# Encoder layer on one core: loads of the first three blocks in one order, and the first turning of results later

## The chip, the cores and the metric

One core of a Trainium2 chip runs the whole program. The metric is the device time of one execution in microseconds (us), the median over runs: 1160.44 us before the change (three runs, 1158.86 to 1162.03).

## What is computed

One layer of an encoder on 256 positions with 2048 features, all in float32:

```python
n = rmsnorm(h, norm_mix_w[layer])
proj = n @ w_in[layer]                       # 2048 x 7168: q_a k_a v_a q_r k_r v_r g_r
attn = dilated_mixture_attention(heads(q_a), heads(k_a), heads(v_a), slopes)
ret = bidirectional_retention(heads(q_r), heads(k_r), heads(v_r), ...)
...
h = h + mixed @ w_out[layer]
n2 = rmsnorm(h, norm_ffn_w[layer])
h = h + (jax.nn.silu(n2 @ w_gate[layer]) * (n2 @ w_up[layer])) @ w_down[layer]
return rmsnorm(h, norm_final_w)
```

## The kernel before

The products make up nearly all of the time. Each float32 factor is split into a high and a low part, and a product is three matmuls (high by high, low by high, high by low). The input projection is cut into seven blocks, `in0` to `in6`, each with 1024 output columns (for `in0` 512 of q_a and 512 of k_a). A block is a string of steps, written out in `ORDERS`. "C" is one K tile taken the plain way: one weight tile of 128 x 1024 (512 KB), 12 matmuls of 512 columns. Numbers 1 to 7 are the products of a Strassen-like scheme for four K tiles (Winograd's), 6 matmuls each. "1a" loads three weight tiles (named rawc, raw12, raw22) and forms sums of them: `rawt` = r11 + r12 on VectorE (DVE), and raw12 += raw22 by an accumulating DMA of GpSimd (POOL). "2a" loads another into raw22, which then takes += rawt in the same way. `in0` has 16 C steps, 192 matmuls. `in1` has seven numbered steps and 12 C, 186 matmuls.

Weights come in the order of the steps over SP's DMA queue, into three buffers rawc, two raw12, three raw22 and one rawt. Each tile is copied by ScalarE (ACT) into its high part, and DVE subtracts to get the low part (`halved`, L154 and L157); the results are `ws` tiles, of which there are five. Preparing runs three steps ahead of the matmuls in program order. x comes transposed in eight pairs of K tiles (`need`), is multiplied by the norm's gain and halved; for the first two pairs, sums of the pair's quarters (`pair_sums`, tiles s and sa) feed the numbered steps. The factor of the norm itself is applied to results afterwards: `measure_x` loads x once more in eight pieces (xs, on POOL's queue), ACT squares and sums each, and `factor` turns the sums into r1 (DVE, DVE, POOL).

The letters M, H, T and N in an order are places for other work. M combines the numbered products. In `in1`, H calls `factor` and scales the four parts of `in0` by r1, and each T turns one part (q, then k) with eight transposes on TensorE (PE) into a bank, from where ACT and DVE halve it. N in `in0` starts `measure_x`. `later` is a list of small pieces of work, one taken after each step.

`ch(ins)` ties an instruction to the one before it on the same engine, so that the scheduler keeps that order. Matmuls, ACT's copies, DVE's steps and POOL's DMAs go through it; SP's loads (L250, L267, L411, L418) do not, and the scheduler places them by its own estimate.

Of the kernel before, what the change touches and what calls it, by code (L numbers as in the profile page):

```python
# [9 lines left out]
F32 = mybir.dt.float32  # L10
F32R = mybir.dt.float32r
AF = mybir.ActivationFunctionType
ALU = mybir.AluOpType
# [75 lines left out]
def encoder_layer(ctx: ExitStack, tc: tile.TileContext, xT, x, gains, gain_f, decay, tab, bias, w_st, y):  # L89
# [49 lines left out]


# [63 lines left out]
    class Block:  # L204


        def __init__(self, name, kind, a, sa, end, hooks=(), parts=None, need=None):
            self.name, self.a, self.sa, self.end, self.hooks = name, a, sa, end, {k: list(v) for k, v in dict(hooks).items()}
            self.parts, self.need, self.fine = parts, need, need is not None
            self.banks, self.raws, self.begun, self.left, self.kept, self.share = {}, {}, set(), {}, [], {}  # L210
            self.steps = steps_of(kind)
            for what, n in self.steps:
                for r in {"C": (2, 3, 4, 8), "K": (2, 3), "Z": ()}.get(what, (what,) if isinstance(what, int) else ()):
                    self.left[r] = self.left.get(r, 0) + (3 if what in ("C", "K") else 6)
                if what == "K":
                    for r in (4, 8):
                        self.left[r] += 3
            stream.extend((self, what, n) for what, n in self.steps)
# [29 lines left out]
        def load(self, home):  # L248
            raw = self.raw(home)
            nc.sync.dma_start(raw, next(tiles).rearrange("p (n c) -> p n c", c=NB))  # L250
            return raw
# [6 lines left out]
        def prepare(self, what, m):  # L258
            if self.need:
                for p in ([m // 2] if what == "C" else [2 * m, 2 * m + 1]):  # L260
                    self.need(p)
            if what == "C" and self.fine:
                self.fine = False
                raw, src = self.raw("c"), next(tiles)
                ws = wsp.tile([P, 2, 2, NB], F32R, tag="ws", name=f"ws_{self.name}")
                for n in range(2):
                    nc.sync.dma_start(raw[:, n], src[:, n * NB:(n + 1) * NB])  # L267
                    copy(ws[:, n, 0], raw[:, n])
                    tt(ws[:, n, 1], raw[:, n], ws[:, n, 0].bitcast(F32), ALU.subtract)
                return ws  # L270
            if what == "C":
                return self.halve(self.load("c"))
# [109 lines left out]
    def end_take(block, i, n, bank):  # L382
        block.share[i, n] = ttile(f"part{i}{n}_{block.name}").rearrange(flat)
# [18 lines left out]
    n1, n1_sums = [None] * (KT // 2), [None] * 2  # L402

    def need(p):
        if n1[p] is not None:
            return
        t = ttile(f"x_{p}")
        w = nw[:, 2 * p:2 * p + 2]
        n1[p] = atile(f"n1_{p}")
        if p < 2:  # L410
            nc.sync.dma_start(t, xT[p])  # L411
            for f in range(2):
                copy(t[:, f], t[:, f], scale=w[:, f:f + 1])
            halved(n1[p], t)
            n1_sums[p] = pair_sums(t, f"n1_{p}")
        else:
            for f in range(2):
                nc.sync.dma_start(t[:, f], xT[p][:, f])  # L418
            weighed(n1[p], t, w)

    def measure_x():
# [11 lines left out]
        for n in range(10):  # L433
            later.append(lambda n=n: (n < 8 and fetch(*divmod(n, 2)), n > 1 and take()))
            later.append(lambda: None)
# [202 lines left out]
    for b, sections in enumerate(INPUT + ((None, None),)):  # L638
        hooks = {}
        if b == 0:  # L640
            hooks = {"N": [measure_x]}
# [17 lines left out]
        if sections[0] is not None:  # L659
            prev = Block(f"in{b}", KIND_IN[b], n1, n1_sums, end_take if b == 0 else end_share if b < 3 else end_scaled, hooks,  # L660
                         need=None if b else need)
# [197 lines left out]
```

## Time and profile before

| | |
|---|---|
| median of 3 runs | 1160.44 us |
| profiled execution | 1162.72 us |
| its span | 1160.9 us |
| PE busy | 1133.2 us (98%), 5166 matmuls |
| DVE, ACT, POOL busy | 923.3, 683.3, 106.5 us |
| HBM read | 223.90 MB, 195 GB/s over the span |

Busy time of PE is modelled and includes matmuls that wait for their input, so the pace of matmuls (starts per microsecond) tells more than the share. "Granted clock" is the share of full speed that the throttle allowed PE.

### The profile page before, as it was taken

The page shows a single profiled execution, that of the slowest core. Times are in us where ns is not written, and L with a number is a line of the kernel's source. Part 1 is how long each engine was busy: PE and PEld are TensorE (multiplying, and loading weights), DVE is VectorE, ACT ScalarE, POOL GpSimd, SP SyncE. Part 2 cuts the span into 40 slices and gives each one's busy share as a digit, 9 for nine tenths or more (in the row PEclk, how much of TensorE's full clock was granted, in tenths as well). Part 3 has the DMA queues.
Part 4 walks back from the last instruction along what each step waited for, and adds up shares of the span by engine and source line. Part 5 has one row for each costly group of instructions (what it writes and reads, how often), then busy time and mean ns, then how long its engine had stood idle before and what let it go on. Part 6 is the DMA issues. An engine that isn't in the chain of part 4 may idle for free.

```text
span 1160.9 us, 14434 instructions
## 1 busy us (share of the span) xinstructions
PE 1133.2 (98%) x5166; PEld 937.8 (81%) x5166; DVE 923.3 (80%) x1052; ACT 683.3 (59%) x842; POOL 106.5 (9%) x135
## 2 busy tenths in 40 slices
PE   8989999999999999999999999999999999999996
PEld 6768888888888887778888888788888888888785
DVE  4658786754577686789998888899989888999895
ACT  4665564745466465656656555576666555666553
POOL 1010100000001110010000021000100202000011
PEclk9899999999999999999999999999999999999999
DMA  8875755455577877669988899988898899889785
GB/s 289 264 209 166 252 181 182 145 171 192 170 250 228 248 201 197 221 191 263 266 248 243 275 261 258 306 240 249 256 274 236 235 323 262 273 260 278 230 233 148
DMA packets 79400, 272.04 MB, mean 234 GB/s; under 512 B 9184, under 2 KB 10720, under 8 KB 79328
## 3 DMA queue, kind: packets, MB, share of 16 engines
q1 hardware_dynamic: 62640, 220.76, 54.7%
q0 software_dynamic: 15968, 49.29, 22.9%
q10 hardware_dynamic: 720, 1.07, 0.3%
q8 instruction: 40, 0.66, 0.2%
q14 instruction: 32, 0.26, 0.1%
HBM read 223.90 MB, written 2.10 MB: 195 GB/s over the span
## 4 chain that ended last, share of the span: by engine, by line
PE 79%; DVE 7%; DMA 6%; ACT 3%; issue 2%; POOL 0%; SPq 0%; DVEq 0%; POOLq 0%; ACTq 0%
PE p_gu L231 32%; PE p_in L231 21%; PE p_d L231 17%; PE p_o L231 5%; DMA rawc_in<-in_w_st 3%; DMA rawc_gu<-in_w_st 2%; DVE ws_gu L157 2%; ACT ws_in L154 1%; DVE ws_in L157 1%; PE pt_h L356 1%; DVE ws_d L157 1%; DMA rawc_o<-in_w_st 1%; ACT ws_gu L154 1%; DMA x<-in_xT 1%; DVE ws_o L157 1%
## 5 line engine op out<-in xcount | busy, mean ns | idle before, releaser
L231 PE MATMUL p_gu<-ws_gu,n 128*128 128x512 f32 x1482 | 351.5, 390 | 3.3 <-ACT ws_gu L154 2.6
L231 PEld LDWEIGHTS p_gu<-ws_gu,n 128*128 128x128 f32 x1482 | 277.7, 188 | 62.3 <-ACT ws_gu L154 3.7
L231 PE MATMUL p_in<-ws_in,n 128*128 128x512 f32 x1284 | 307.9, 397 | 6.2 <-ACT ws_in L154 6.2
L231 PEld LDWEIGHTS p_in<-ws_in,n 128*128 128x128 f32 x1284 | 242.6, 191 | 57.3 <-ACT ws_in L154 7.7
L157 DVE TENSOR_TENSOR ws_in<-rawc_in,ws_in 128x1024 fp32r<-128x1024 f32 (+1 forms) x107 | 129.0, 1212 | 68.2 <-ACT ws_in L154 67.0
L231 PE MATMUL p_d<-ws_d,h 128*128 128x512 f32 x708 | 168.0, 390 | 0.9 <-DVE ws_d L157 0.9
L157 DVE TENSOR_TENSOR ws_gu<-rawc_gu,ws_gu 128x1024 fp32r<-128x1024 f32 x113 | 137.6, 1221 | 28.0 <-ACT ws_gu L154 26.5
L231 PEld LDWEIGHTS p_d<-ws_d,h 128*128 128x128 f32 x708 | 132.7, 188 | 29.3 <-DVE ws_d L157 1.3
L154 ACT ACTIVATE ws_gu<-rawc_gu 128x1024 fp32r<-128x1024 f32 x113 | 118.7, 1055 | 54.9 <-PE p_gu L231 28.4
L154 ACT ACTIVATE ws_in<-rawc_in 128x1024 fp32r<-128x1024 f32 (+1 forms) x107 | 111.6, 1047 | 66.1 <-PE p_in L231 44.2
L231 PE MATMUL p_gu<-ws_gu,sa_n 128*128 128x512 f32 x504 | 128.7, 391 | 0.0
L231 PEld LDWEIGHTS p_gu<-ws_gu,sa_n 128*128 128x128 f32 x504 | 93.9, 188 | 19.4 <-DVE ws_gu L157 0.4
L157 DVE TENSOR_TENSOR ws_gu<-raw_gu,ws_gu 128x1024 fp32r<-128x1024 f32 x84 | 102.4, 1220 | 2.4 <-ACT ws_gu L154 1.1
L154 ACT ACTIVATE ws_gu<-raw_gu 128x1024 fp32r<-128x1024 f32 x84 | 88.5, 1053 | 23.1 <-PE p_gu L231 18.5
L157 DVE TENSOR_TENSOR ws_d<-rawc_d,ws_d 128x1024 fp32r<-128x1024 f32 x54 | 65.7, 1220 | 17.6 <-ACT ws_d L154 17.0
L154 ACT ACTIVATE ws_d<-rawc_d 128x1024 fp32r<-128x1024 f32 x54 | 57.1, 1057 | 37.2 <-PE p_d L231 20.1
L154 ACT ACTIVATE ws_gu<-rawt_gu 128x1024 fp32r<-128x1024 f32 x42 | 44.3, 1055 | 56.4 <-DVE rawt_gu L157 41.9
L231 PE MATMUL p_d<-ws_d,sa_h 128*128 128x512 f32 x240 | 61.2, 390 | 0.0
L157 DVE TENSOR_TENSOR ws_gu<-rawt_gu,ws_gu 128x1024 fp32r<-128x1024 f32 x42 | 51.3, 1221 | 5.6 <-ACT ws_gu L154 5.6
L231 PEld LDWEIGHTS p_d<-ws_d,sa_h 128*128 128x128 f32 x240 | 44.8, 188 | 9.2
L154 ACT ACTIVATE ws_d<-raw_d 128x1024 fp32r<-128x1024 f32 x40 | 42.2, 1056 | 12.1 <-PE p_d L231 11.1
L157 DVE TENSOR_TENSOR ws_d<-raw_d,ws_d 128x1024 fp32r<-128x1024 f32 x40 | 48.8, 1219 | 0.6
(186 smaller groups left out, 1138.7 us busy)
## 6 DMA issues: line engine op xcount, KB each, us to landing
rawc_gu<-in_w_st SPq DMA_DIRECT2D x113, 512.0 KB, 5.3
rawc_in<-in_w_st SPq DMA_DIRECT2D x105, 512.0 KB, 4.2
raw_gu<-in_w_st SPq DMA_DIRECT2D x63, 512.0 KB, 5.3
rawc_d<-in_w_st SPq DMA_DIRECT2D x58, 512.0 KB, 5.0
raw_d<-in_w_st SPq DMA_DIRECT2D x30, 512.0 KB, 4.9
rawc_o<-in_w_st SPq DMA_DIRECT2D x26, 512.0 KB, 4.9
raw_gu<-raw_gu POOLq DMA_DIRECT2D x21, 512.0 KB, 7.2
raw_gu<-rawt_gu POOLq DMA_DIRECT2D x21, 512.0 KB, 5.3
```

The source lines that it names most:

```text
L154: ch(nc.scalar.activation(out, src, func, **kw))
L157: ch(nc.vector.tensor_tensor(out, x, y, op=op))
L231: ch(nc.tensor.matmul(self.bank(r), x[u], w[v], start=r not in self.begun, stop=self.left[r] == 0))
L356: ch(nc.tensor.transpose(pt[:, f, i * P:(i + 1) * P], t(i)[:, (2 * p + f) * P:(2 * p + f + 1) * P], ident))
```

## The change

- SP's loads of `in0`, `in1` and `in2` go through `ch`, so they leave in the order in which the program names them. Until now the scheduler put some tiles of `in1` and `in2` in front of x.
- x comes in eight loads of 256 KB, each named between the weight tiles that use it, and is multiplied and halved one K tile at a time, directly from the loaded tile. The weighed x for the sums of the first two pairs is rebuilt as high + low on DVE.
- `measure_x` starts after 11 steps of `in0`, not after 4, and its pieces are then taken one after each step, not one in two.
- In `in1`, H and the two T stand after M; the parts of `in0` are kept in other buffers (`resp`).
- A small ACTIVATE on `mhalf` stands ahead of all others.

```diff
-    "in0": "C C C C N C C C C C C C C C C C C",
-    "in1": "1a 5a C 2a C 3a C H C T C T C 6a C 7a M C C 4a C C C",
+    "in0": "C C C C N C C C C C C C N C C C C C",
+    "in1": "1a 5a C 2a C 3a C C 6a C 7a M C H C C T C T 4a C C C",
...
+    nc.scalar.activation(mhalf, mhalf, AF.Copy)
...
-            nc.sync.dma_start(raw, next(tiles).rearrange("p (n c) -> p n c", c=NB))
+            load = nc.sync.dma_start(raw, next(tiles).rearrange("p (n c) -> p n c", c=NB))
+            if self.early:
+                ch(load)
...
-                    nc.sync.dma_start(raw[:, n], src[:, n * NB:(n + 1) * NB])
+                    ch(nc.sync.dma_start(raw[:, n], src[:, n * NB:(n + 1) * NB]))
+                fetch_x(1)
+                part_x(0, 0)
+                for n in range(2):
                     copy(ws[:, n, 0], raw[:, n])
                     tt(ws[:, n, 1], raw[:, n], ws[:, n, 0].bitcast(F32), ALU.subtract)
                 return ws
+            if self.opens:
+                raw = self.load("c")
+                if m % 2 == 0 and m < KT - 2:
+                    fetch_x(m // 2 + 1)
+                part_x(m // 2, m % 2)
+                return self.halve(raw)
...
+    def fetch_x(p):
+        xt[p] = ttile(f"x_{p}")
+        ch(nc.sync.dma_start(xt[p], xT[p]))
+
+    def part_x(p, f):
+        w = nw[:, 2 * p + f:2 * p + f + 1]
+        if f == 0:
+            n1.append(atile(f"n1_{p}"))
+        copy(n1[p][:, f, 0], xt[p][:, f], scale=w)
+        stt(n1[p][:, f, 1], xt[p][:, f], w, n1[p][:, f, 0].bitcast(F32), ALU.mult, ALU.subtract)
+
+    def sums_n1():
+        for p in range(2):
+            t = ttile(f"xw_{p}")
+
+            def weigh(p=p, t=t):
+                tt(t, n1[p][:, :, 0].bitcast(F32), n1[p][:, :, 1].bitcast(F32), ALU.add)
+
+            later.append(weigh)
+            n1_sums.append(pair_sums(t, f"n1_{p}"))
...
-        for n in range(10):
-            later.append(lambda n=n: (n < 8 and fetch(*divmod(n, 2)), n > 1 and take()))
-            later.append(lambda: None)
+        for n in range(11):
+            later.append(lambda n=n: (n < 8 and fetch(*divmod(n, 2)), n > 2 and take()))
```

On SP, from the third weight tile of `in0` on, the queue before holds tiles of `in1` and `in2` ahead of x pairs 2 and 3 (rawc_in0 are the weights of `in0`, x_2 is the third pair; the last number is only an instruction's number):

```order
L250 DMA rawc_in0_127<-in_w_st 128x1024
L250 DMA raw12_in1_440<-in_w_st 128x1024
L250 DMA rawc_in0_132<-in_w_st 128x1024
L250 DMA rawc_in0_173<-in_w_st 128x1024
L250 DMA rawc_in0_192<-in_w_st 128x1024
L250 DMA raw22_in1_442<-in_w_st 128x1024
L418 DMA x_2_165<-in_xT 128x256 x2
L250 DMA rawc_in0_221<-in_w_st 128x1024
L250 DMA raw22_in1_506<-in_w_st 128x1024
L250 DMA raw12_in2_796<-in_w_st 128x1024
L250 DMA rawc_in0_240<-in_w_st 128x1024
L418 DMA x_3_213<-in_xT 128x256 x2
```

and now, from the same tile on:

```order
L252 DMA rawc_in0_119<-in_w_st 128x1024
L417 DMA x_2_121<-in_xT 128x512
L252 DMA rawc_in0_129<-in_w_st 128x1024
L459 DMA rates_89<-in_decay 128x16
L252 DMA rawc_in0_160<-in_w_st 128x1024
L417 DMA x_3_162<-in_xT 128x512
L252 DMA rawc_in0_182<-in_w_st 128x1024
L252 DMA rawc_in0_201<-in_w_st 128x1024
L417 DMA x_4_203<-in_xT 128x512
```

x_2 stood behind five tiles after the third weight tile, two of them of `in1`; now it is the next load, and nothing of `in1` goes out before all of `in0`.

On POOL, where block `in0` passes into `in1`, the loads of x for the squares (xs00 to xs31) and the two weight additions stood as follows before:

```order
L427 DMA xs00_257<-in_x 128x512
L427 DMA xs01_301<-in_x 128x512
L427 DMA xs10_345<-in_x 128x512
L427 DMA xs11_390<-in_x 128x512
L427 DMA xs20_435<-in_x 128x512
L176 DMA raw12_in1_440<-raw22_in1_442 128x1024
L427 DMA xs21_478<-in_x 128x512
L176 DMA raw22_in1_506<-rawt_in1_447 128x1024
L427 DMA xs30_519<-in_x 128x512
L427 DMA xs31_553<-in_x 128x512
```

and now:

```order
L442 DMA xs00_405<-in_x 128x512
L442 DMA xs01_426<-in_x 128x512
L178 DMA raw12_in1_430<-raw22_in1_432 128x1024
L442 DMA xs10_452<-in_x 128x512
L442 DMA xs11_470<-in_x 128x512
L442 DMA xs20_496<-in_x 128x512
L178 DMA raw22_in1_499<-rawt_in1_437 128x1024
L442 DMA xs21_512<-in_x 128x512
L442 DMA xs30_527<-in_x 128x512
L442 DMA xs31_549<-in_x 128x512
```

Five of eight xs loads stood ahead of the first addition, now two, and three stand behind the second addition as before xs21 did not.

On ACT the squares stand between the copies of `in1`'s weights. Now, from step 2a's copy (ws_in1_501) to that of 6a (ws_in1_582, from rawt):

```order
L156 ACTIVATE ws_in1_501<-raw22_in1_499 128x2x512
L156 ACTIVATE xs10_452,sums_x_93<-xs10_452 128x512
L156 ACTIVATE ws_in1_517<-rawc_in1_515 128x2x512
L156 ACTIVATE xs11_470,sums_x_93<-xs11_470 128x512
L156 ACTIVATE ws_in1_530<-raw22_in1_432 128x2x512
L156 ACTIVATE xs20_496,sums_x_93<-xs20_496 128x512
L156 ACTIVATE ws_in1_554<-rawc_in1_552 128x2x512
L156 ACTIVATE xs21_512,sums_x_93<-xs21_512 128x512
L156 ACTIVATE ws_in1_566<-rawc_in1_564 128x2x512
L156 ACTIVATE xs30_527,sums_x_93<-xs30_527 128x512
L156 ACTIVATE ws_in1_582<-rawt_in1_437 128x2x512
```

where before there stood, from step 2a's copy (ws_in1_508) on:

```order
L154 ACTIVATE ws_in1_508<-raw22_in1_506 128x2x512
L154 ACTIVATE xs20_435,sums_x_93<-xs20_435 128x512
L154 ACTIVATE ws_in1_524<-rawc_in1_522 128x2x512
L154 ACTIVATE ws_in1_534<-raw22_in1_442 128x2x512
L154 ACTIVATE xs21_478,sums_x_93<-xs21_478 128x512
L154 ACTIVATE ws_in1_558<-rawc_in1_556 128x2x512
L154 ACTIVATE ws_in1_569<-rawc_in1_567 128x2x512
L154 ACTIVATE xs30_519,sums_x_93<-xs30_519 128x512
```

A square now stands ahead of each copy there, where it stood ahead of every second one; xs21 is ahead of the copy for the fourth C (ws_in1_566).

## Rows read from the trace of the kernel before

**Rows 1.** The page: busy time of the engines, and the 40 slices of PE and of its granted clock, in tenths.

```profile
PE 1133.2 (98%) x5166; PEld 937.8 (81%) x5166; DVE 923.3 (80%) x1052; ACT 683.3 (59%) x842; POOL 106.5 (9%) x135
...
PE   8989999999999999999999999999999999999996
PEclk9899999999999999999999999999999999999999
```

**Rows 2.** The timeline of PE: start in us, length of the group in us, engine, line, operation, result and operands, count, and in brackets the idle time before it with what ended it. sa_n operands belong to numbered steps (5a at 62.20 in in1, 5a at 112.45 in in2), pt_q, pt_k are the turning.

```profile
7.07 13.84 PE L231 MATMUL p_in<-ws_in,n 128*128 128x512 f32 x48 [1.98 <-ACT ws_in L154]
21.97 5.73 PE L231 MATMUL p_in<-ws_in,n 128*128 128x512 f32 x24 [1.07 <-ACT ws_in L154]
30.84 31.52 PE L231 MATMUL p_in<-ws_in,n 128*128 128x512 f32 x126 [3.13 <-ACT ws_in L154]
62.20 1.52 PE L231 MATMUL p_in<-ws_in,sa_n 128*128 128x512 f32 x6
...
81.05 2.37 PE L356 MATMUL pt_q<-ident,part_in 128*128 128x128 f32 x8 [3.73 <-ACT part_in L154]
...
96.13 16.48 PE L231 MATMUL p_in<-ws_in,n 128*128 128x512 f32 x72
112.45 1.52 PE L231 MATMUL p_in<-ws_in,sa_n 128*128 128x512 f32 x6
...
164.02 1.04 PE L356 MATMUL pt_q<-ident,part_in 128*128 128x128 f32 x8
164.81 3.01 PE L231 MATMUL p_in<-ws_in,n 128*128 128x512 f32 x12
```

**Rows 3.** Short stretches: busy time and instruction count of each engine, then the granted clock, the DMA share and GB/s.

```profile
7.50:10.00 2.50, 2.50 (x7) 1.95 (x7) 1.58 (x3) 1.78 (x4) 0.00 (x0) 1.00 1.04 408
...
12.50:15.00 2.50, 2.50 (x12) 2.03 (x11) 1.63 (x3) 1.06 (x1) 0.00 (x0) 1.00 0.72 239
...
30.00:32.50 2.50, 1.66 (x4) 1.37 (x5) 2.04 (x3) 2.50 (x4) 0.54 (x1) 0.50 0.98 320
32.50:35.00 2.50, 2.50 (x7) 1.92 (x7) 2.50 (x5) 1.50 (x3) 0.13 (x1) 0.50 0.78 229
35.00:37.50 2.50, 2.50 (x10) 1.94 (x9) 0.72 (x2) 1.11 (x2) 0.40 (x1) 0.68 0.85 264
...
80.00:85.00 5.00, 3.81 (x14) 3.20 (x15) 1.18 (x2) 4.72 (x7) 0.24 (x1) 0.66 0.35 105
```

**Rows 4.** The chain that ended last: start and length in us, and what it was.

```profile
2.12 6.12 DMA rawc_in<-in_w_st
...
13.87 6.17 DMA x<-in_xT
...
41.21 5.55 DMA rawc_in<-in_w_st
...
49.21 4.28 DMA rawc_in<-in_w_st
...
68.03 8.65 DMA rawc_in<-in_w_st
```

**Rows 5.** The timeline of the other engines, in columns as in rows 2; SPq is SP's queue of loads, xs the loads and squares of x.

```profile
3.64 1.28 ACT L154 ACT_TABLE_LOAD   x1 [3.64 <-DMA x<-in_xT]
4.93 0.91 ACT L154 ACTIVATE x<-x,nw 128x256 f32<-128x256 f32 x2
...
8.45 4.88 SPq L250 DMA_DIRECT2D rawc_in<-in_w_st  x3
...
12.76 1.06 ACT L154 ACTIVATE ws_in<-rawc_in 128x1024 fp32r<-128x1024 f32 x1 [1.04 <-DMA rawc_in<-in_w_st]
...
38.87 1.06 ACT L154 ACTIVATE ws_in<-rawc_in 128x1024 fp32r<-128x1024 f32 x1 [0.61 <-DMA rawc_in<-in_w_st]
...
53.60 1.06 ACT L154 ACTIVATE ws_in<-rawc_in 128x1024 fp32r<-128x1024 f32 x1 [0.88 <-DMA rawc_in<-in_w_st]
54.69 1.23 DVE L157 TENSOR_TENSOR ws_in<-rawc_in,ws_in 128x1024 fp32r<-128x1024 f32 x1 [1.32 <-ACT ws_in L154]
...
64.80 1.41 POOL L427 DMA_DIRECT2D xs<-in_x  x2
...
72.70 0.63 ACT L154 ACTIVATE xs<-xs 128x512 f32<-128x512 f32 x1 [4.92 <-DMA xs<-in_x]
...
80.28 2.56 ACT L154 ACTIVATE part_in<-part_in,r 128x512 f32<-128x512 f32 x4 [1.82 <-POOL r L200]
```

**Rows 6.** Up to 120 us and kept apart by shape, groups of instructions (busy us, mean ns of one), an issue's line (KB each, median us to landing), and for the tiles raw_in and xs, in this order, the us from a load's issue to its landing.

```profile
L154 ACT ACTIVATE n<-x,nw 128x256 fp32r<-128x256 f32 x12 | 5.5, 498 | 11.7 <-DMA x<-in_xT 11.7
L160 DVE SCALAR_TENSOR_TENSOR n<-x,nw,n 128x256 fp32r<-128x256 f32 x12 | 5.4, 480 | 8.1 <-ACT n L154 8.1
L154 ACT ACTIVATE part_in<-p_in 128x512 f32<-128x512 f32 x5 | 2.6, 589 | 0.0
L154 ACT ACTIVATE ws_in<-rawc_in 128x512 fp32r<-128x512 f32 x2 | 1.1, 613 | 0.0
...
rawc_in<-in_w_st SPq DMA_DIRECT2D x2, 256.0 KB, 3.9
...
DMA to landing us min/median/max: 5.9/7.2/8.8
...
DMA to landing us min/median/max: 4.2/6.1/9.3
```

More of the change, by code (lines that the diff above doesn't have):

```diff
@@ L204, in encoder_layer, with __init__ @@
     class Block:
-        def __init__(self, name, kind, a, sa, end, hooks=(), parts=None, need=None):
+        def __init__(self, name, kind, a, sa, end, hooks=(), parts=None, opens=False, early=False):
             self.name, self.a, self.sa, self.end, self.hooks = name, a, sa, end, {k: list(v) for k, v in dict(hooks).items()}
-            self.parts, self.need, self.fine = parts, need, need is not None
+            self.parts, self.opens, self.early = parts, opens, early
             self.banks, self.raws, self.begun, self.left, self.kept, self.share = {}, {}, set(), {}, [], {}
@@ L258, in prepare @@
         def prepare(self, what, m):
[L259 to L263, printed above, removed]
+            if self.opens and m == 0:
                 raw, src = self.raw("c"), next(tiles)
@@ L382, in end_take @@
     def end_take(block, i, n, bank):
-        block.share[i, n] = ttile(f"part{i}{n}_{block.name}").rearrange(flat)
+        if not block.kept:
+            block.kept += [resp.tile([P, 2, NB], F32, tag="res", name=f"part{k}_{block.name}") for k in range(2)]
+        block.share[i, n] = block.kept[i][:, n]
         copy(block.share[i, n], bank)
@@ L399, in end_share @@
         tt(block.share[i, n], bank, block.share[i, n], ALU.add)
[L402 to L419, printed above, removed]
+    xt, n1, n1_sums = {}, [], []
+    def fetch_x(p):
[14 more added lines that the diff above has]
+            n1_sums.append(pair_sums(t, f"n1_{p}"))
     def measure_x():
@@ L640, in encoder_layer @@
         if b == 0:
-            hooks = {"N": [measure_x]}
+            fetch_x(0)
+            hooks = {"N": [sums_n1, measure_x]}
         else:
@@ L660, in encoder_layer @@
             prev = Block(f"in{b}", KIND_IN[b], n1, n1_sums, end_take if b == 0 else end_share if b < 3 else end_scaled, hooks,
-                         need=None if b else need)
+                         opens=b == 0, early=b < 3)
             (sec, prev.half), _ = sections
```

## The prediction

> **What bounds the kernel now.** I read the page's slices first [rows 1]. TensorE (PE) is busy in 98% of the span and its slices are all nines after the first three; only those first slices, some 90 us, show an 8, and the granted clock dips in slice 2. So I went to the timeline of PE [rows 2] and measured pace there instead of busy time. Between 96.13 and 112.45 us 72 matmuls start (step 5a of in2 opens behind them), which is 0.2267 us each. A classical step "C" (12 matmuls) is thus worth 2.72 us of PE, a numbered step (6) 1.36 us. Eight transposes are worth 0.79 us (164.02 to 164.81).
>
> Block in0 is 192 matmuls, 43.5 us at that pace. It runs from 7.07 us to 60.84 us (the first matmul with sa_n, at 62.20, less the six of step 1a): 53.8 us, 10.3 too many. Four pieces account for nearly all of it. PE was idle 1.07 us before 21.97 and 3.13 us before 30.84 [rows 2]. The granted clock is 0.50 from 30 to 35 us and 0.68 in the next 2.5 us [rows 3]: the lower of the two levels lasted until about 36.6 us, so 5.8 us of work ran at half pace, 2.9 us lost. And at the very start only 7 matmuls are counted in the 2.5 us from 7.5 where 12 come from 12.5 us on [rows 3]; the clock column says 1.00 there, but the pace is that of the lower level. If it held from 7.07 to 12.7 us it covers 12.4 matmuls, and the other 35.6 of the 48 end at 20.8 us; the row says 7.07+13.84 = 20.91. So steps 1 to 4 of in0 are limited by that pace and not by data, at 2.8 us lost.
>
> Block in1 is 186 matmuls and 16 transposes, 42.2 + 1.6 = 43.8 us. It takes from 60.84 to 111.09 (112.45 less step 1a of in2), 50.3 us, 6.5 too many: 3.73 us idle before the transposes at 81.05 [rows 2], 1.7 us at half pace after that (granted 0.66 over 80 to 85 us [rows 3]), 1.1 us of small change. Both blocks together hold 16.8 us that a better order could give back; beyond 112 us I expect nothing to move.
>
> What ended the waits stands in the chain [rows 4]. The x tile of pair 2 is loaded from 13.87 to 20.04; SP (the load queue) could issue it no earlier since three weight loads in front of it waited for buffers, from 8.45 to 13.33 [rows 5]. In in1 the sum of squares is late: two xs loads issued from 64.80 let ScalarE (ACT) start its square only at 72.70 after 4.92 us of waiting, a weight load issued at 68.03 took 8.65 us, and its halving, the reduction, the root and the scaling of the parts follow in one chain until 81.05 [rows 4, 5].
>
> **The change part by part.**
> *Start.* The table load of 1.28 us waited for x until 3.64 [rows 5]; with an ACTIVATE of its own it runs while x travels. x then needs one copy of half a tile (0.50) and one VectorE (DVE) step of 0.48 in place of two copies and a full tile's halving [rows 6]. So n1 is ready at about 3.64 + 0.50 + 0.48 = 4.6 us, and the first weight half decides: issued at 1.18, 3.9 us to land [rows 6], 5.1, plus its copy of 0.61 [rows 6] is 5.7 us. That is 1.4 earlier than 7.07. Bounds: no gain, if the half lands only when the first matmul could start before, and 2.3 us if it is there as soon as x is copied (4.14 + 0.61). I take 1.4.
>
> The row shows one ACT_TABLE_LOAD of 1.28 us, with the copy of x starting 0.01 us behind it [rows 5]. The Trainium skill (ScalarE: Activation LUTs, What ACT_TABLE_LOAD costs) adds a drain of about 1.38 us to each load and counts some 2.66 us. By that figure the first matmul could come 1.4 us sooner still; the row leaves no room for a drain, and the first weight half would hide it.
>
> *Block in0, loads in order.* All bytes are as before; x comes in eight DMAs of 256 KB where it had two and twelve of half the size. Is PE fed? Weight tile k+3 can be issued once DVE has read tile k (three buffers). For tile 3: tile 0 is read by about 7.2 us (two halvings on DVE behind 5.7), the row's load took 4.3 us (8.45 to 12.76 [rows 5]), so it is copied at 7.2 + 4.3 + 1.06 = 12.6 us. After that the tiles of before, fed with x, xs and weights mixed, came from 38.87 to 53.60 six steps apart, 2.45 us each [rows 5]; a cycle of 4.28 to 5.55 us of load [rows 4] and 2.32 us of copy and halving (53.60 to 55.92 [rows 5]), divided by three buffers, is 2.2 to 2.6. Both lie under the 2.72 us that PE needs. Tile 15 is then copied at 12.6 + 12 x 2.45 = 42.0 us. PE, with the slow pace for 5.6 us again, reaches 11.3 us with 12.4 matmuls and needs 40.7 us for the other 179.6: end 52.0 us, tile 15 wanted at 49.3. Seven microseconds of stock, so neither the two gaps nor the dip behind them come back: 60.84 - 52.0 = 8.8 us gained. Bounds: if the zero matmuls that open PE now run into the real ones without the idle time before 7.07 and the clock is up at once, tile 1 decides (landed 8.24 [rows 4], copied 9.3) and the block ends at 9.3 + 15 x 2.72 = 50.1. If every load took the 7.2 us of the raw tiles [rows 6], a step would be 3.17 us, tile 15 copied at 50.7 and the end 53.4.
>
> The two additions that rebuild weighed x for the sums (about 0.6 us each on DVE, half of a weight tile's 1.23 [rows 5]) and the one-step-at-a-time x work leave DVE 1.23 + 0.48 us per step plus these, under 2.72: nothing. The loads of in1 and in2 that used to go out early no longer stand in front of x, but they now have to come in time.
>
> *Block in1.* Step 1a needs three tiles at once. Tile 13 is read at 12.6 + 10 x 2.45 + 1.25 = 38.4 us; then the three go out, 5 to 7.2 us each [rows 4, 6], and are there by 46.5, when PE wants them at 52.0 and 53.4. The three tiles after these (first C, 2a, second C) land by about 50.4. That is in time. What is late is xs: POOL now has six of its eight loads behind the two weight additions (raw12 += raw22, and raw22 += rawt). The first addition can go when DVE has read raw12, about 47.2; an issue takes POOL 0.7 (1.41 for two at 64.80 [rows 5]), so the next three xs go from 47.9. The second needs step 2a's tile halved on ACT and DVE. ACT first copies the four parts of in0 (from 52.0, 0.59 each [rows 6]) and a square, so the tile is read by 57.4; then comes the addition, and the last three xs go from 58.1. ACT stands in order: square xs21 is ahead of the copy for the fourth C. With the 7.9 us from 64.80 to 72.70 it lands at 66.0; square with its accumulator 0.8 and copy 1.06 make 67.9. PE wants it at 52.0 + 60 x 0.2267 = 65.6. With 6.1 us (the median) the copy ends at 66.1, with 9.3 (the longest) at 69.3 [rows 6]. I take 67.7, near the row that has additions and xs side by side, so a stall of 2.1 us; between 1.07 us, which did not lower the clock, and 3.13, which did [rows 2, 3], I assume it does not.
>
> *Factor and turning, later.* All squares are then done well before the factor. Four scalings (2.56 us in all at 80.28 [rows 5]) have two C steps, 5.4 us, to hide behind, and with step M done four banks are free for the transposed tiles. The 3.73 us and the slow pace behind it go. If that cover failed, the same 3.73 + 1.7 would be back. At the join to in2 the first tiles are now issued after the last of in1, but about six C steps ahead of use: nothing.
>
> **Sum.** in1 ends at 67.7 + 126 x 0.2267 + 1.6 = 97.9 us, before 111.1: 13.2 us gained. The profiled execution took 1162.7 us (span 1160.9 and 1.8 around it), so this one would take 1149.5; it is 2.3 above the median of the runs, 1160.4, from which the same gain gives 1147.2. I predict 1147.5.
>
> **The rivals.**
> *Loads put late cost more than they save.* In before xs were issued at leisure and four tiles of in1 and in2 were fetched in in0. The Trainium skill says to issue a DMA early and wait for it late (DMA: Bandwidth & Descriptors, Rules for kernel authors); the change does the opposite with these. Worked out from rows: xs21 takes 9.3 us, the fourth C starts at 69.3, the stall of 3.7 us is longer than the 3.13 that went with a lower clock, and 1.7 to 2.9 us of half pace follow. The same 9.3 us for xs10 in front of the second C add 0.3. in1 ends at 101.2 to 102.7: gain 8.4 to 9.9, 1150.5 to 1152. For it: the 8.65 us row. Against it: xs in before took 6.1 as a median.
>
> *Better than forecast.* in0 ends at 50.1 and xs land in 4.2 to 6.1 us: the fourth C starts at 63.7 to 66.1, in1 ends at 93.9 to 96.3, gain 15 to 17, and 1.0 more where the first half lands early: 1142 to 1145.5.
>
> *Slower.* One queue in strict order, with three buffers and nothing fetched ahead, makes every step wait for a load's full time. Were that time the 8.65 us of the row at 68.03 through both blocks, a step is (8.65 + 2.32)/3 = 3.66 us; in0 ends at 12.6 + 12 x 3.66 + 2.7 = 59.2 and in1 after 12 such steps, 9.5 us of numbered steps and 1.6 of transposes at 114.2: 3.1 slower, about 1163.5, more with the clock down. It decides from 3.53 us a step, loads of 8.3 us. Against it: 4.28 to 5.55 us in the same stretch of before [rows 4].
>
> **How the numbers follow.** Forecast, gain 10 to 15 us (1145.5 to 1150.5): 0.57. Late loads: 0.18. Better: 0.15. Slower, or so close to it that the gain is under 3.5 us: 0.08, of it 0.03 slower by over 0.3%. The rest, 0.02, is a gain between. 0.3% of 1160.4 is 3.5 us, about what a measurement here can tell from none. Range 1141.5 to 1154.5: it takes in the better and the late case.
>
> **What would show it.** First matmul of in0 near 5.7 us, no idle time of PE over 1 us until in0 ends, first sa_n matmul at 53 to 54 (was 62.20), no clock of 0.50 between 20 and 50 us. ACT waiting for xs in in1, PE idle about 2 us before a C near 66; no wait at the transposes; the first sa_n matmul of in2 near 99 (was 112.45). Wrong if ACT waits for weight tiles in in0 with PE idle behind it, if PE idles 3 us or more in in1 with a granted clock under 1 behind it, or if anything past in2 moves.

## The result and the profile after

The changed kernel took 1148.68 us (median of four runs, 1148.03 to 1150.28) beside 1160.81 us for the kernel before in the same session: a ratio of 0.9893, 95% interval [0.9876, 0.991], 12.1 us less. The forecast was 1147.5. The profiled execution took 1148.03 us (span 1146.2), 14.7 less than that of before; the forecast gave 13.2 between such executions.

The page after, with the lines that answer to [rows 1]:

```profile
PE 1127.6 (98%) x5166; PEld 935.5 (82%) x5166; DVE 924.2 (81%) x1056; ACT 681.9 (59%) x841; POOL 106.5 (9%) x135
...
PE   9999999999999999989999999999999999999996
...
PEclk9999999999999999999999999999999999999999
```

The 8s of the first slices are gone. A new 8 stands in slice 18, from 487 to 516 us, far from anything that the change names. The timeline of PE, in the columns of [rows 2], shows the start, the opening of in1 (51.60 is its step 5a), the turning, and in2's step 5a (95.61):

```profile
1.31 3.49 PE L787 MATMUL p_in<-zero 128*128 128x512 f32 x8 [1.31 <-POOL zero L125]
5.04 3.33 PE L233 MATMUL p_in<-ws_in,n 128*128 128x512 f32 x12 [0.23 <-ACT ws_in L156]
9.27 42.50 PE L233 MATMUL p_in<-ws_in,n 128*128 128x512 f32 x186 [0.90 <-ACT ws_in L156]
51.60 1.52 PE L233 MATMUL p_in<-ws_in,sa_n 128*128 128x512 f32 x6
...
80.17 1.04 PE L365 MATMUL pt_q<-ident,part_in 128*128 128x128 f32 x8
...
95.61 1.52 PE L233 MATMUL p_in<-ws_in,sa_n 128*128 128x512 f32 x6
```

PE has one run of 186 matmuls where [rows 2] had gaps of 1.07 and 3.13 us, and no bracket stands at the turning, where 3.73 us of idle time stood. The step 5a of in1 starts at 51.60 (before 62.20) and that of in2 at 95.61 (before 112.45). So 16.8 us were gained by in2, more than were left at the end.

The short stretches, columns as in [rows 3], say the same of the pace:

```profile
7.50:10.00 2.50, 1.60 (x7) 1.01 (x6) 0.75 (x1) 1.84 (x3) 0.00 (x0) 1.00 0.95 354
10.00:12.50 2.50, 2.50 (x13) 2.02 (x12) 2.44 (x5) 2.10 (x4) 0.00 (x0) 1.00 0.58 138
...
32.50:35.00 2.50, 2.50 (x12) 2.07 (x12) 2.43 (x6) 0.07 (x1) 0.00 (x0) 1.00 0.93 319
...
80.00:85.00 5.00, 5.00 (x32) 4.30 (x31) 3.74 (x4) 5.00 (x8) 0.00 (x0) 1.00 0.10 20
```

The full pace, 12 or 13 in 2.5 us, is there from 10 us on, and the clock stays at 1.00 where it was 0.50 and 0.66. The 7 matmuls of the first row are a gap of 0.90 us behind a fast first step, not half pace. The chain [rows 4] has become one load and one long run of PE:

```profile
2.59 5.54 DMA rawc_in<-in_w_st
9.27 71.07 PE p_in L233 x312
```

That load is weight tile 1: it decides the second step of in0. The other engines, in the columns of [rows 5], ACT first and then POOL, whose two additions are the raw_in lines:

```profile
1.18 1.28 ACT L140 ACT_TABLE_LOAD   x1 [1.18 <-PEq L867]
2.48 0.20 ACT L140 ACTIVATE mhalf<-mhalf 128x4 f32<-128x4 f32 x1
3.80 0.51 ACT L156 ACTIVATE n<-x,nw 128x256 fp32r<-128x256 f32 x1 [1.12 <-DMA nw<-in_gains]
...
8.16 1.06 ACT L156 ACTIVATE ws_in<-rawc_in 128x1024 fp32r<-128x1024 f32 x1 [2.00 <-DMA rawc_in<-in_w_st]
...
40.75 1.06 ACT L156 ACTIVATE ws_in<-rawc_in 128x1024 fp32r<-128x1024 f32 x1 [1.09 <-DMA rawc_in<-in_w_st]
...
54.50 0.63 ACT L156 ACTIVATE xs<-xs 128x512 f32<-128x512 f32 x1 [1.49 <-DMA xs<-in_x]
...
77.71 2.56 ACT L156 ACTIVATE part_in<-part_in,r 128x512 f32<-128x512 f32 x4 [3.67 <-POOL r L202]
```

```profile
47.08 0.89 POOL L178 DMA_DIRECT2D raw_in<-raw_in  x1 [18.68 <-DVE rawt_in L159]
47.64 1.96 POOL L442 DMA_DIRECT2D xs<-in_x  x3
54.56 0.90 POOL L178 DMA_DIRECT2D raw_in<-rawt_in  x1 [4.96 <-DVE ws_in L159]
55.13 1.97 POOL L442 DMA_DIRECT2D xs<-in_x  x3
```

The table load now runs ahead of x. The scalings (77.71) end at 80.27, just as the turning begins. The square of xs10 (54.50) waited 1.49 us for its load and cost PE nothing in this execution.

Of the 16.8 us, 3.1 were lost in the stretch of gu0, the first block of the feed-forward part, and 1.2 came back near the end. Two places in that stretch differ: its start, and the first transposes of its results, pt_h, some 50 us later. PE and ACT of the kernel after, and then of before:

```profile
444.35 4.61 PE L233 MATMUL p_gu<-ws_gu,n 128*128 128x512 f32 x12 [1.57 <-ACT ws_gu L156]
...
479.91 1.06 ACT L156 ACTIVATE ws_gu<-rawc_gu 128x1024 fp32r<-128x1024 f32 x1 [3.67 <-DMA rawc_gu<-in_w_st]
...
495.53 0.33 PE L365 MATMUL pt_h<-ident,part_gu 128*128 128x128 f32 x1 [2.56 <-DVE part_gu L162]
496.19 1.76 PE L365 MATMUL pt_h<-ident,part_gu 128*128 128x128 f32 x7 [0.34 <-DVE part_gu L162]
```

```profile
461.32 3.04 PE L231 MATMUL p_gu<-ws_gu,n 128*128 128x512 f32 x12 [1.57 <-ACT ws_gu L154]
...
494.91 1.06 ACT L154 ACTIVATE ws_gu<-rawc_gu 128x1024 fp32r<-128x1024 f32 x1 [1.58 <-PE p_gu L231]
...
510.53 0.33 PE L356 MATMUL pt_h<-ident,part_gu 128*128 128x128 f32 x1 [0.66 <-DVE part_gu L160]
511.20 0.98 PE L356 MATMUL pt_h<-ident,part_gu 128*128 128x128 f32 x7 [0.34 <-DVE part_gu L160]
```

The short stretches at both places, of after and then at pt_h of before, have the granted clock in the third column from the right:

```profile
446.00:448.00 2.00, 2.00 (x6) 1.62 (x5) 1.67 (x2) 2.00 (x5) 0.00 (x0) 0.50 0.88 242
496.00:498.00 2.00, 1.81 (x8) 1.81 (x9) 1.85 (x3) 2.00 (x3) 0.00 (x0) 0.50 0.22 88
```

```profile
511.00:513.00 2.00, 1.80 (x12) 1.63 (x13) 1.86 (x3) 2.00 (x3) 0.00 (x0) 1.00 0.21 86
```

At the start the same idle of 1.57 us stands in both kernels, and behind it the 12 matmuls take 4.61 us in one, at the lower clock, and 3.04 in the other. This looks like the loss, but it isn't: before then waits 1.2 us at transposes some 10 us on, and from the start of the stretch to just ahead of pt_h after took 91.37 us and before 91.60. The 3.1 us are lost at pt_h. There the next 34 matmuls and transposes take 11.61 us in place of 8.23: PE waits 1.9 us longer (2.56 and 0.66), and the clock drops to 0.50 behind that wait. The wait reaches back to ACT's row: in after the copy at 479.91 waited for its weight tile, which took 4.9 us from issue to landing; in before that tile took 3.4 us, and what released its copy last was PE.

### The profile page after: what moved, and what is told of

Its sections match the earlier page's. It is cut to its first block, busy times and chain, and to the rows that moved or that the text cites. A ratio compares the mean times of both kernels' runs of the same rounds, so it can differ in the third digit from the quotient of the medians.

```text
span 1146.2 us, 14428 instructions
## 1 busy us (share of the span) xinstructions
PE 1127.6 (98%) x5166; PEld 935.5 (82%) x5166; DVE 924.2 (81%) x1056; ACT 681.9 (59%) x841; POOL 106.5 (9%) x135
## 3 DMA queue, kind: packets, MB, share of 16 engines
q10 hardware_dynamic: 720, 1.07, 0.3%
## 4 chain that ended last, share of the span: by engine, by line
PE 83%; DVE 6%; DMA 5%; issue 3%; ACT 2%; POOL 0%; SPq 0%; DVEq 0%; POOLq 0%; ACTq 0%
PE p_gu L233 35%; PE p_in L233 26%; PE p_d L233 13%; PE p_o L233 5%; DMA rawc_d<-in_w_st 2%; DMA rawc_gu<-in_w_st 2%; DVE ws_d L159 2%; DVE ws_gu L159 2%; PE pt_h L365 1%; DMA rawc_o<-in_w_st 1%; DVE ht L159 1%; ACT ws_gu L156 1%; DVE ws_o L159 1%; PE ps_sa L482 1%; PE ps_oa L493 1%
## 5 line engine op out<-in xcount | busy, mean ns | idle before, releaser
L233 PE MATMUL p_in<-ws_in,n 128*128 128x512 f32 x1284 | 302.0, 391 | 1.2 <-ACT ws_in L156 1.1
L233 PEld LDWEIGHTS p_in<-ws_in,n 128*128 128x128 f32 x1284 | 238.2, 188 | 50.4 <-ACT ws_in L156 2.5
```

Of the source, the lines that this page charges most:

```text
L233: ch(nc.tensor.matmul(self.bank(r), x[u], w[v], start=r not in self.begun, stop=self.left[r] == 0))
```

## The experiments

My theory after the result: ordering the loads feeds PE through in0; late turning takes its wait away; the squares of xs, which stand ahead of weight copies on ACT, are the weak place; and what was given back at gu0 is chance of an execution, not the change. The rivals: the new loads of x and the finer steps on it (not the order) did it; the early first matmul lets the clock rise; the loss at gu0 belongs to the changed order.

This table has one profiled execution of each kernel, from the starts of matmuls in the traces (us). in0 and in1 are the lengths of these blocks, from first matmul to the next block's first; matmuls, transposes among them, are counted from in0's first as number 0, the zero matmuls left out; the stretch of gu0 goes from number 1900 to 2392, the last column from 4200 to the last matmul.

| kernel | first matmul | in0 | in1 | gu0 | end |
|---|---|---|---|---|---|
| before | 7.07 | 53.77 | 50.25 | 113.88 | 216.86 |
| e11, before again | 7.24 | 52.61 | 50.84 | 117.11 | 214.69 |
| after | 5.04 | 45.21 | 44.01 | 117.03 | 215.61 |
| e0, after again | 5.08 | 45.47 | 45.03 | 112.74 | 214.59 |
| e5, chain only | 7.15 | 45.36 | 48.47 | 113.05 | 215.59 |
| e2, loads free | 5.00 | 45.08 | 47.08 | 114.34 | 214.43 |
| e1, turned early | 4.94 | 44.79 | 51.99 | 113.25 | 214.63 |
| e7, later output squares | 4.98 | 44.74 | 48.04 | 114.49 | 214.53 |
| e4, no early ACTIVATE | 5.99 | 44.51 | 44.83 | 115.31 | 214.79 |
| e6, one zero matmul | 5.34 | 46.07 | 43.95 | 114.67 | 216.25 |
| e8, e12, squares later | 5.13, 4.96 | 44.78, 46.04 | 43.95, 43.95 | 115.04, 114.07 | 214.55, 214.56 |
| e9, with x's pair later | 5.10 | 44.79 | 43.95 | 112.99 | 216.67 |
| e10, squares sooner | 5.03 | 45.32 | 45.71 | 113.63 | 214.51 |

Between in2's first matmul and number 1900 all took 305.2 to 306.4 us, and from 2392 to 4200 404.7 to 404.9. The end of 216.86 us in before is 214.69 in e11, the same kernel, so the 1.2 us that came back there are no gain of the change either.

### What the order of loads is worth

**e5_chain_only** is the kernel before with `ch` on SP's loads of the first three blocks and nothing else.

```diff
-            nc.sync.dma_start(raw, next(tiles).rearrange("p (n c) -> p n c", c=NB))
+            load = nc.sync.dma_start(raw, next(tiles).rearrange("p (n c) -> p n c", c=NB))
+            if self.early:
+                ch(load)
...
-            nc.sync.dma_start(t, xT[p])
+            ch(nc.sync.dma_start(t, xT[p]))
```

> The kernel before with nothing but the chain on SP's loads of the first three blocks (x halves in the same chain). If the order alone feeds in0, the gaps of 1.07 and 3.13 us and the dip of the clock behind them go (7 us), the slow start of 2.8 us and the wait at the transposes stay or move by a few us: 1152 to 1155, first sa_n matmul of in1 at 55 to 56. If the finer steps on x are needed too, in0 keeps idle time and the time is 1157 to 1161.

It took 1151.33 us, ratio 0.9905 [0.9888, 0.9922]. Its PE timeline:

```profile
7.15 46.88 PE L231 MATMUL p_in<-ws_in,n 128*128 128x512 f32 x198 [2.09 <-ACT ws_in L154]
...
70.94 0.33 PE L358 MATMUL pt_q<-ident,part_in 128*128 128x128 f32 x1 [1.95 <-ACT part_in L154]
...
76.73 1.25 PE L358 MATMUL pt_k<-ident,part_in 128*128 128x128 f32 x8 [1.42 <-DVE q L157]
```

The order alone makes in0 one run: both gaps and the dip behind them go, and in1 starts at 52.51, 8.3 of the 10.6 us that the whole change gains there. The rest is the earlier first matmul, 5.04 in place of 7.15; in0 is as long in both (45.21 and 45.36). The waits at the turning stay (1.95, 0.28 and 1.42 us), but without the lower clock behind them that before had. Time and start of in1 (its 5a at 53.87) are a little better than was expected. So the order is enough to feed PE in in0; e2 asks whether it is needed.

**e2_sp_free** is the changed kernel without `ch` on SP's loads; x is still named early.

```diff
-            if self.early:
-                ch(load)
...
-        ch(nc.sync.dma_start(xt[p], xT[p]))
+        nc.sync.dma_start(xt[p], xT[p])
```

> The changed kernel without the chain on SP's loads: the scheduler again puts raw12, raw22 of in1 and one raw12 of in2 between the tiles of in0, but x pairs 3 and 4 now stand early of themselves. If the single order is what feeds in0, idle time of over 2 us and a clock of 0.50 come back in in0 and the time is 1155 to 1159. If the place of x in the queue is what counts, in0 runs without idle time over 1 us, the first matmul of in1 stands at 50 to 51 us, and the time is 1147 to 1150.

It took 1148.18 us, 0.9881 [0.9863, 0.9899], as the changed kernel. Three tiles of later blocks again went out ahead of in0's last (at 15.8, 22.1 and 30.7 us), but x stood far enough in front, and in0 took 45.08. So it isn't needed: either edit makes x come in time, and the second adds little to the first. In in1 this profile shows waits of 0.20, 0.21 and 1.01 us, the last behind a square of xs as in e7 below, and a length of 47.08; whether the chain is worth something there the medians don't tell.

### The start

**e4_table_late** leaves out the small ACTIVATE. **e6_one_zero** opens with one zero matmul, where eight keep PE at work until 4.8 us; the zeros are no part of the result.

```diff
-    nc.scalar.activation(mhalf, mhalf, AF.Copy)
```

```diff
-            for n in range(8):
+            for n in range(1):
```

> The changed kernel without the small ACTIVATE at the start, so that the table load waits for x or the gains. Theory: the first matmul comes 1.0 to 1.3 us later (about 6.1 us, 5.035 in the changed kernel), but in0's second step is decided by the landing of tile 1 (copied at 9.2 us), so in1 starts at 50.2 to 50.6 and the time is that of the changed kernel within 0.5 us. Rival: the early first matmul is what lets the clock rise in time; then the slow pace lasts into the second step, in1 starts at 51 to 53 and the time is 1 to 2 us longer.

> The changed kernel with one zero matmul at the start in place of eight, so that PE stands still from about 2 us to the first real matmul at 5.0. Theory: what PE does just ahead of in0's first matmul sets its pace there; without the zeros it runs at half pace as in the kernel before (12 matmuls in about 5.5 us instead of 3.3, and so on to 10 or 11 us), in0 ends 1 to 2 us later, in1 starts at 51 to 52. Rival: the pace at the start comes with the time since launch; then nothing changes, in1 starts at 50.2.

e4 took 1146.65 us, 0.9875 [0.9851, 0.99]; its first matmul came at 5.99, 0.95 later than after's, and in1 started at 50.50, 0.26 later: the theory. Its median lies 0.9 us over that of the unaltered kernel in the same session (e0, 1145.72), within the intervals of both. The early table load is worth 0.95 us at the first matmul and next to nothing a step later, since tile 1 decides there. PE timelines of e4, and then of e6 with its short stretches:

```profile
5.99 3.07 PE L232 MATMUL p_in<-ws_in,n 128*128 128x512 f32 x12 [1.14 <-ACT ws_in L155]
```

```profile
1.32 0.80 PE L787 MATMUL p_in<-zero 128*128 128x512 f32 x1 [1.32 <-POOL zero L125]
5.34 7.02 PE L233 MATMUL p_in<-ws_in,n 128*128 128x512 f32 x19 [3.22 <-ACT ws_in L156]
```

```profile
7.50:10.00 2.50, 2.50 (x7) 1.92 (x7) 0.87 (x1) 1.96 (x3) 0.00 (x0) 1.00 0.99 381
10.00:12.50 2.50, 2.50 (x11) 2.01 (x11) 2.48 (x5) 2.14 (x4) 0.00 (x0) 1.00 0.58 142
```

With the idle of 3.22 us ahead of its first matmul, e6 shows the half pace of before, 7 in 2.5 us with no gap, until about 10 us, and in1 starts at 51.41, 1.2 later than after's. With idle of 0.23 us (after) and 1.14 (e4) the first twelve take 3.33 and 3.07 us. The other profiles fall into the same two groups: in the ten with eight zeros and at most 1.14 us of idle behind them, the starts of matmuls show full pace by 7.4 us, and in1 starts at 49.72 to 51.00; in the four with 1.98 to 3.22 us (before, e11, e5, e6) half pace lasts until 10.2 to 12.4 us. So it is what PE does ahead of the first real matmul that sets the pace behind it. e6 has one run, 1148.09 us.

The Trainium skill (ScalarE: Activation LUTs, What ACT_TABLE_LOAD costs) adds a drain to the load. No run here shows one: in after the load ends at 2.46 and the next ACTIVATE starts at 2.48.

### The turning

**e1_turn_early** is the changed kernel with in1's order as before.

```diff
-    "in1": "1a 5a C 2a C 3a C C 6a C 7a M C H C C T C T 4a C C C",
+    "in1": "1a 5a C 2a C 3a C H C T C T C 6a C 7a M C C 4a C C C",
```

> The changed kernel with the two turnings and the scaling of in1 back at their old place (after the third C), all else as changed. If the turning's place was worth what the wait of before shows (3.73 us idle and 1.7 us at half pace), PE waits 3 us or more at the transposes and the time is 1153 to 1155. If the earlier end of the squares (64.8 us instead of 78.5) already removes that wait, PE idles 0 to 1.5 us there and the time is 1148.5 to 1150.5.

It took 1150.45 us, 0.9902 [0.9883, 0.992]. Its waits at the transposes lie between the two expectations. The PE timeline has two separate losses in in1:

```profile
59.30 4.51 PE L233 MATMUL p_in<-ws_in,n 128*128 128x512 f32 x12 [2.62 <-ACT ws_in L156]
...
71.69 0.33 PE L365 MATMUL pt_q<-ident,part_in 128*128 128x128 f32 x1 [1.07 <-ACT part_in L156]
...
77.48 1.25 PE L365 MATMUL pt_k<-ident,part_in 128*128 128x128 f32 x8 [1.43 <-DVE q L159]
```

The first, at the second C, has nothing to do with the turning: e7 below, which turns late, has it too (2.17 us, with the lower clock behind it in both). In e1 in1 took 51.99 us, in e7 48.04; less the 0.45 by which e1's stall is longer, 3.5 us are what the late turning is worth in these two profiles. In the medians the intervals of the two overlap.

### The squares of x

**e7_out_squares** delays the squares of the output block by one step; until 400 us its program is that of the changed kernel.

```diff
         o = ht[block.q + n][:, i]
         tt(o, bank, o, ALU.add)
+        if i + n == 0:
+            later.append(lambda: None)
```

> The changed kernel with the squares after the output blocks put one step later, so that ACT copies the next weights first and doesn't wait 3.3 us for DVE at the start of gu0 (442.6 us). If the 3.4 us that the changed kernel lost again near 495 us come from the idle time and the clock of 0.50 near 445 us, the idle time there shrinks to under 1 us, the clock stays up, PE waits about 1 us instead of 2.9 before the first transposes of h, and the time is 1144.5 to 1146. If they come from the loads of gu0, nothing changes there and the time is 1147.5 to 1149.5.

It took 1147.66 us, 0.9878 [0.986, 0.9895]. PE at gu0's start waits 0.73 and 0.93 us in place of 1.57, and 0.55 before pt_h, as the first case expected. But e0, e1, e2 and e12 wait as little there (0.60 to 0.83) without this edit, and the table has gu0 at 114.49, among the others: the edit settles nothing about gu0. In in1, which it doesn't touch, PE stalled. PE's timeline, ACT's at that time, and the chain:

```profile
58.86 4.61 PE L233 MATMUL p_in<-ws_in,n 128*128 128x512 f32 x12 [2.17 <-ACT ws_in L156]
```

```profile
57.14 0.63 ACT L156 ACTIVATE xs<-xs 128x512 f32<-128x512 f32 x1 [3.70 <-DMA xs<-in_x]
57.67 0.19 ACT L156 ACTIVATION_READ_ACCUMULATOR xs<-xs 128x1 f32 x1
57.76 1.04 ACT L156 ACTIVATE ws_in<-rawc_in 128x1024 fp32r<-128x1024 f32 x1
```

```profile
48.08 9.04 DMA xs<-in_x
```

xs10 took 9.04 us to land, its square waited on ACT, and the weight copy behind it, whose tile is the second C's, came 2.17 us too late. So one program gave two executions. **e0_again**, the changed kernel unaltered, put that to the test.

> The changed kernel, unchanged, once more. Theory: where xs10 lands is left to chance (landings of 6.7 to 9.2 us seen), and a PE idle of 1.6 to 2.6 us sometimes lowers the granted clock for 3.4 us and sometimes not. Then the profile may show a stall at in1's second C and another count of dips in gu0/gu1 than the first profile of the same program did, and the time stays at 1147.5 to 1150. Rival: the stall and the dip belong to the program; then this profile shows no idle over 1 us in in1 and a granted clock of 0.50 behind the idle at gu0's start again, at 443 to 449 us.

It took 1145.72 us (1142.74 to 1150.4, six runs), 0.9862 [0.9836, 0.9888], below the expected 1147.5 to 1150. Its profile has ACT waiting 3.17 us for xs10, PE idle 0.78 us behind it, and a full clock after the idle at gu0's start:

```profile
58.29 3.02 PE L233 MATMUL p_in<-ws_in,n 128*128 128x512 f32 x12 [0.78 <-ACT ws_in L156]
...
445.30 3.02 PE L233 MATMUL p_gu<-ws_gu,n 128*128 128x512 f32 x12 [1.55 <-ACT ws_gu L156]
```

Both halves of the theory hold: stall and dip vary between executions of one program. **e8_take_later** moves the squares, not the loads, three steps back; **e12_take_again** is the same kernel once more.

```diff
-        for n in range(11):
-            later.append(lambda n=n: (n < 8 and fetch(*divmod(n, 2)), n > 2 and take()))
+        for n in range(14):
+            later.append(lambda n=n: (n < 8 and fetch(*divmod(n, 2)), n > 5 and take()))
```

> The changed kernel with each square of xs taken three steps later, so that no square waiting for xs10 stands ahead of the copy for in1's second C. Theory: no idle of PE over 1 us in in1, whatever the landing of xs10; the factor is then still ready before the scaling (M is followed by H), in2 starts at 93.5 to 94.5, and the median is 0.5 to 2 us under the changed kernel's (about 1147). Rival: the squares taken late push the factor behind H, PE waits at pt_q for 1 us or more, and the time is not under the changed kernel's.

> The kernel with squares taken three steps later once more. Theory: no stall in in1 in this execution either, in2 starts at 93.3 to 94.5; the median is 1143 to 1146, and a spread between executions remains from gu0 and gu1. Rival: the 17.2 us of the first profile at in2 were a lucky landing; then in1 shows an idle of 1.5 us or more, in2 starts at 96 or later and the median is that of the changed kernel, 1146 to 1149.

They took 1143.92 and 1145.76 us, 0.9846 [0.9824, 0.9868] and 0.9868 [0.9853, 0.9883]. in1 took 43.95 us in both, against 43.8 for its matmuls and transposes alone, without a wait of PE. (In e12 in2 still started at 94.94, past the expected 94.5, as its in0 lost 1.45 us waiting for tile 1.) With the squares in their old place an execution can have luck and lose nothing either: in1 took 44.01 us in after and 43.95 in e6. e12 shows why its 43.95 isn't a lucky landing, from the xs tile's view (us from issue to landing):

```profile
DMA to landing us min/median/max: 5.4/10.3/11.9
```

The loads were slower than in after (3.9, 6.4 and 8.2) and PE did not feel it. The Trainium skill (DMA: Bandwidth & Descriptors, Rules for kernel authors) says to issue a DMA early and wait for it late; this edit does only the second half, and the trace agrees: 43.95 us in both profiles of it, in place of 43.95 to 48.04 with the squares in their old place.

**e10_n_earlier** starts loads and squares three steps sooner instead.

```diff
-    "in0": "C C C C N C C C C C C C N C C C C C",
+    "in0": "C C C C N C C C C N C C C C C C C C",
```

> The changed kernel with measure_x started after 8 steps of in0 in place of 11: three xs loads stand ahead of the first weight addition on POOL, and every square comes three steps sooner. Theory (late xs10 beside the weight loads is what stalls in1): xs are then in flight beside in0's own weight loads; the stall at in1's second C goes, or moves a step with another xs. No idle over 1 us if xs land in under 7 us, in1 starts within 0.5 us of 50.2, in2 at 93.5 to 95, median 1144 to 1147. Rival: each square has the same one or two steps between its load and its place, so it only moves the wait into in0 or step 1a; PE then idles 1 us or more there and the time is that of the changed kernel or more.

It took 1148.44 us, 0.989 [0.9873, 0.9906], and PE stands 1.47 us before the same C: the square of another xs, of one that was loaded at 49.1 us, now stands in its way. The place differs from the rival's, the reason and the time are its own: as far as one profile shows, the distance between load and square matters, not the start.

**e9_all** takes e8's and e7's edits and loads x's second pair behind weight tile 1.

```diff
-                fetch_x(1)
...
+                if m == 1:
+                    fetch_x(1)
```

> Squares of xs three steps later, one empty piece ahead of the output block's squares, and x's second pair loaded behind weight tile 1. Theory: no stall in in1, the second step of in0 starts up to 1 us earlier (tile 1 lands before 7.5 us in place of 8.1), in0 ends at 49 to 50 us, the median is 1.5 to 3 us under the changed kernel's (1145.5 to 1147). Rival: x's second pair now comes late and PE idles over 1 us in steps 3 or 4 of in0; then in1 starts at 50.5 or later and nothing is gained over the kernel with the squares alone.

It took 1144.29 us, 0.9847 [0.9826, 0.9868], better than was expected but no better than e8. in0 has no gap at all in its profile, but in1 starts at 49.89 against e8's 49.91: its first matmuls run at half pace until 7.4 us, longer than e8's.

### The stretch at gu0

**e11_before_again** is the kernel before, unaltered.

> The kernel before, unchanged, profiled once more. Theory: the 10 us lost in in0, and the waits at the transposes of in1, belong to its order and come again (in1 starts at 60 to 61.5, in2 at 110 to 112.5); whether the idle of about 1.5 us at gu0's start lowers the clock is left to chance. Rival: its gaps at 21.97 and 30.84 were chance as well; then in1 starts under 58 us and the total is 3 us or more shorter.

One run, 1163.42 us. Its gaps in in0 and at the turning are there again (in1 starts at 59.85). At gu0, where the first profile of before kept its clock and waited 0.66 us, it shows what the changed kernel showed:

```profile
460.43 4.61 PE L231 MATMUL p_gu<-ws_gu,n 128*128 128x512 f32 x12 [1.57 <-ACT ws_gu L154]
...
496.10 1.06 ACT L154 ACTIVATE ws_gu<-rawc_gu 128x1024 fp32r<-128x1024 f32 x1 [3.44 <-DMA rawc_gu<-in_w_st]
...
511.72 0.33 PE L356 MATMUL pt_h<-ident,part_gu 128*128 128x128 f32 x1 [2.56 <-DVE part_gu L160]
```

The stretch takes 117.11 us here, 113.88 in the first profile of before, 117.03 and 112.74 in the two of the changed kernel. What seemed to be given back is the spread of either kernel.

The fourteen profiles also tell where the spread comes from. In four (after, e11, e4, e8) the weight tile of ACT's row took 4.1 to 5.1 us to land and PE waited 2.22 to 2.56 us at pt_h; in the other ten it took 3.4 to 3.5 us and PE waited at most 1.35. In two of the four (after, e11) the clock fell behind the wait, which makes them the longest. Each of the three kernels that were profiled twice has one execution of either kind: after and e0, e11 and before, e8 and e12. The lower clock at gu0's start, however, leaves nothing behind: up to number 2140, among the transposes some 10 us on, the stretch took 55.63 to 56.78 us in the six profiles that had it and 55.23 to 56.67 in the six that kept the clock behind the same idle. That the late tile is the cause is read from these rows; no run moved it, and why it lands late stays open.

## Why the prediction was right, point by point

**The time** was right, 1147.5 between the two measured medians of 1148.68 and 1145.72, but the execution that I compared with got there by two errors against each other.

**Start.** Forecast 5.7 us, measured 5.04: too late by 0.7, inside its bounds. e4 shows the part of the table load, 0.95 us. It hardly mattered, as tile 1 decides the next step (copied at 8.16 to 9.22; the bound had 9.3).

**in0, "with the slow pace for 5.6 us again".** This step failed. Forecast end 52.0, measured 50.24; I had named the bound, 50.1, for a start without idle time, and it is that case. e6 shows the other: with 3.22 us of idle, in1 starts 1.2 us later. Taken from row to row: idle of 1.98 us (before), 2.09 (e5), 2.14 (e11) and 3.22 (e6) is followed by half pace until 10 us or later, 0.23 and 1.14 are not. The change took that idle away, and I kept its consequence.

**in0, fed by loads in order.** Right. Tile 15 was copied at 40.75 to 41.81 (forecast 42.0) and wanted about 47.5, one C before 50.24: nearly six microseconds of stock. Both gaps and the dip are gone, and e5 shows that the order of the loads alone does it (and e2 that x named early does it too).

**in1, the stall of 2.1 us "before the fourth C", by xs21.** The mechanism was right, the place wrong, the size a matter of chance. It is the second C, by xs10, and in five further profiles with the squares placed so (e0, e4, e2, e7, e1) PE stood 0.78, 0.59, 1.01, 2.17 and 2.62 us there; in after, and in e6, not at all. The place follows from the step before: I had xs10 landing after 9.3 us cost 0.3 with in0 ending at 52.0, and as in0 ended 1.8 earlier the same landing costs 2.0. The assumption that such a stall leaves the clock up fell too: in e7 and e1 it went down. The first addition and the three loads behind it went at 47.08 and 47.64, where I had 47.2 and 47.9; the last three loads, xs21 first, at 55.13, where I had 58.1, and xs21 kept PE waiting in none of these profiles.

**Factor and turning, later.** Right: no wait, the scalings done at 80.27 as PE came to the turning. Forecast 3.73 + 1.7 = 5.4 us; e1 against e7 shows 3.5: PE waits 1.07, 0.28 and 1.43 us at an early turning, and no lower clock follows.

**"Beyond 112 us I expect nothing to move."** Wrong as a statement on an execution, and the step that the forecast time owes most to; the prediction itself had named anything that moves past in2 as a sign of being wrong. Of the 3.7 us by which in2 began earlier than forecast (94.25 against 97.9), 3.1 were lost at pt_h in gu0. e0 and e11 show that the loss isn't the change's. I took a single profile's wait and clock there for a property of the program. That the forecast lay so near the time of this execution is in part luck.

**The rivals.** Slower did not come near. Late loads came true in e7 and e1 in their mechanism, at another C, but e7 took 1147.66 us and not 1150.5 to 1152. Better than forecast is, within 0.3 us, e0 (a gain of 15.4 us in medians) and, with the squares moved, e8.

**What may beat both kernels** is e8: the profiles show its mechanism in three of three (e8, e12, e9), and its median lies 1.8 us under e0 in the same session; but the intervals of e8 and e12 both overlap that of e0, and e12's median, 1145.76, is e0's 1145.72, so its lead over the changed kernel in time isn't settled.

## What to carry to other kernels

When PE starves early while its share is 98%, look at the order in which the load queue really issues: one chain on the loads gave 8.3 of 10.6 us here. An instruction that waits for a DMA makes everything behind it on its engine wait, so keep its issue and move its use back (e8), not both (e10). And before you book a gain or a loss of 3 us, profile the same kernel twice.

## What was not expected of the hardware

The same idle of PE at gu0's start, 1.55 to 1.57 us, was followed by a granted clock of 0.50 in six of twelve profiles (after, e1, e2, e6, e10, e11) and by none in the other six (before, e0, e4, e5, e8, e12), with nothing in the order between them that would tell which, and with no loss left from it at the transposes some 10 us on. A weight tile that took 1.5 us longer to land went with 1.9 us more of waiting, 15 us on (after beside before). xs loads of 256 KB beside weight loads landed after 3.8 to 11.9 us. At the start, the clock column reads 1.00 while 7 matmuls in 2.5 us show half pace (e6); there the pace is to be trusted, not the column. In e5 the column does show it, at 0.66 over 7.5 to 12.5 us.
